# Gate tiles of the recurrent branch: from eight plain projections to a stage of block products

## The chip, the cores and the metric

The kernel runs on one core of one Trainium2 chip. The core has five engines with a queue each: TensorE (PE; its weight loads are listed apart as PEld), VectorE (DVE), ScalarE (ACT), GpSimd (POOL) and SyncE (SP), which here only issues DMAs. An engine works through its queue in order; an instruction whose input is not ready holds up all that stands behind it on that engine. SBUF holds tiles of 128 partitions; PE writes its sums into PSUM, eight banks of 128 x 512 floats here. The metric is the device time of one execution in microseconds (us), lower is better, taken as the median of several runs.

## The reference

One layer over a sequence of 1024 positions and 1024 channels. The input is normalised and modulated (`h`), and one combined projection `h @ w_in` gives the inputs of two branches and of the merge gates:

```python
hq, hf, hi, hz, gq, gk, gv, gz, ga, mg = jnp.split(h @ w_in[l], IN_OFFSETS, axis=-1)
y_h = hgrn2_branch(hq, hf, hi, hz, ...)   # 8 heads; o = linear recurrence;  rms_norm(o) * silu(hz)
y_g = gla_branch(gq, gk, gv, gz, ga, ...) # 4 heads; per-head rms_norm(o) * silu(gz)
u_h = y_h @ w_branch[l, 0]
u_g = y_g @ w_branch[l, 1]
mg = jax.nn.sigmoid(mg.reshape(B, T, 2, D_MODEL))
merged = mg[:, :, 0] * u_h + mg[:, :, 1] * u_g
x = x + gate[:, None, :] * (merged @ w_out[l])
```

and a final RMS norm. The change is about `hz`: the gate input of the recurrent branch, 1024 x 1024 like each half of `mg`. The output `o` of the recurrent branch is normalised over all 1024 channels, so the normalising factor of a position is known only when all eight heads are done; `silu(hz)` multiplies element by element and can come before or after it.

## The kernel before

All matrix products keep float32 accuracy by splitting both operands into a high and a low part of a faster type and adding three products (high x high, high x low, low x high). ACT makes the high part, DVE the low part (`split`, L195 is DVE's half).

The work has two long stretches. In the first, `Stream.go` runs a list of jobs: projections of 128 output channels (`Feat`, L454: 8 blocks of the inner dimension x 3 products x 2 halves of the sequence = 48 matmuls of 512 columns) and value blocks (`Vblk`, `Vblk2`). For each of the eight recurrent heads the list has `hq`, `hf` and, last, `hz`; for `hz` `silu_done` makes the Silu of the finished projection with a Sigmoid on ACT (L865) and a product on DVE (L866). After every six matmuls or so a job yields, and `Stream.weave` (L808) then lets two side tracks go on: `side`, the attention of the heads one after another (`attention`, L565), and `back`, preparations. Each track is a generator that yields a number of units, its distance to its next step; `PACE` = 1.1 is how many units of the side track pass with each yield of the main work. So the attention's small matmuls and its long DVE chains are spread between the projection matmuls, and where a head's steps stand in PE's queue is decided when the program is built (a scheduler may still shift an instruction by its own estimate of readiness).

A head's steps in PE's order: first score products (L596), second (L628), third (L683, L689, L694), transposes of the keys (L720), state updates (L742), outputs (L761, L763). Between them DVE multiplies in decay factors: `L592` must be done before the first step, `L624` before the second, `L672` before the third, `L748` makes the states that the outputs read. In the recurrent branch `post` then takes each half of the output out of PSUM: ACT squares it (L1007), DVE multiplies it by the norm weight and by the Silu'd gate tile (L1008), and POOL's queue stores the product to DRAM (`yh_d`, L829). POOL adds up the squares (L1019). After the eighth head `root_mean` splits the sum, adds over partitions by matmuls with `ones_r` (L876, L877), takes the root (L878), and DVE the reciprocal (L1028): the factors `rst_h`.

The back track holds `prepare`: differences of the quarters of `h` (`factors`, L1140) and sums of weight quarters (`weight_sums`, L1169 to L1173) for the second stretch, stored to DRAM by POOL (L1175). `gate_side` sums the output gate from the conditioning vector (L966), from its own place on the back track.

The second stretch, `last_stages`, computes four 1024 x 1024 products by a block scheme: each product is cut into 2 x 2 blocks and seven block products take the place of eight (`PRODUCTS`; their operands are sums and differences of quarters). A stage is 7 block products x 4 pairs of output tiles (`Pair`) x 12 matmuls = 336 matmuls (L1317). The stages in order: the gate of branch 1 (`put_gate1`), the gate of branch 0 (`put_gate0`), the branch product of `y_g` (`put_t1`) and of `y_h` (`put_m`). The first two use the same left operand `h`, so its split factors (`H[0, p]`, L1237, L1238) are kept from the first to the second. Weights come in pairs, are split by ACT (L1259) and DVE (L1260) two ahead. Before the last stage `scale_quad` (L1216) multiplies the quarters of `y_h` by `rst_h`. The side track's last head runs on inside the first stage; `scores_done` and `side_done` make PE's remaining PSUM banks (the score tile, the small tiles) available to the stages, and `seed` fills a bank with an earlier partial result.

The slot pool `S` (46 slots of 4 KB per partition) hands out all large SBUF tiles.

Of the kernel before, what the change touches and what calls it, by code (L numbers as in the profile page):

```python
# [9 lines left out]
F32 = mybir.dt.float32  # L10
# [16 lines left out]
PACE = 1.1  # L27
# [55 lines left out]
def hybrid_trunk_kernel(  # L83
# [686 lines left out]
    class Stream:  # L770


        def __init__(self):
            self.jobs = []
            self.loaded = self.prepped = 0
            self.side = deque()
            self.back = deque()
            self.hooks = {}

# [28 lines left out]
        def weave(self, units):  # L808
            for track, pace in ((self.side, PACE), (self.back, 1)):
# [188 lines left out]
    def hgrn_attention(h):  # L998
# [4 lines left out]
        def post(vh, half, po):  # L1003
            if half == 0:
                y[0], sq[0] = st.pop(("z", h)), S.get([T])
            sl = slice(half * 512, half * 512 + 512)
            nc.scalar.activation(sq[0][:, sl], po, AF.Square)  # L1007
            nc.vector.scalar_tensor_tensor(y[0][:, sl], po, vec[:, R_HN + h:R_HN + h + 1],  # L1008
                                           y[0][:, sl], ALU.mult, ALU.mult)
# [22 lines left out]
    def hgrn_v(h):  # L1032
        def done(v):
            h_state[("v", h // 4)] = v
            if h == 0:
                stream.back.append([gate_side(), 4])
        J.append(Vblk2(C_HI + h * P, done, lambda: start_side(hgrn_attention(h), 4)))

    for h in range(8):
# [9 lines left out]
        J.append(Feat(col(C_HZ + h * P), rhs_h, silu_done(h_state, ("z", h))))  # L1049
# [102 lines left out]
    sources = [[col(C_MG + n * D + d * P, 2 * P) for d in range(0, 8, 2)] for n in (1, 0)]  # L1152
    sources += [[branch(n, d) for d in range(0, 8, 2)] for n in (1, 0)]

    w_sums = [[[dp.tile([P, T], F32, name=f"ws{b}{j}{i}") for i in range(4)] for j in range(2)] for b in range(4)]
# [35 lines left out]
    GROUPS = [(b, p) for b in range(4) for p in PRODUCTS]  # L1191
    BUILT = [g for g in GROUPS if g[0] != 1]
# [3 lines left out]
    acts_of = {2: yg_d, 3: yh_d}  # L1196
    QUAD = {1: "11", 2: "21", 3: "22", 5: "11", 6: "22", 7: "12", 4: "21"}
    outs = [None] * 4
# [11 lines left out]

    def scale_quad(b, z):
        half = int(z[1]) - 1
        rst = rst_h[0][:, half * 512:half * 512 + 512].unsqueeze(1).to_broadcast([P, 2, 512])
        for t in quads[b, z]:
            v = t.rearrange("p (a t) -> p a t", a=2)
            nc.vector.tensor_mul(v, v, rst)  # L1216
# [8 lines left out]
    def build(g):  # L1225
# [4 lines left out]
        srcs = raw_f.pop(g) if b < 2 else quads[b, QUAD[p]]  # L1230
        for kk, src in enumerate(srcs):
# [7 lines left out]
            if b < 2:  # L1239
                S.free(src)  # L1240
        if b >= 2 and p in (7, 4):
# [39 lines left out]
    class Pair:  # L1281
# [25 lines left out]
        def run(self, p):  # L1307
# [4 lines left out]
            h = H[0 if self.b == 1 else self.b, p]  # L1312
# [48 lines left out]
    pairs = {(b, i): Pair(b, i) for b in range(4) for i in range(4)}  # L1361

    def last_stages():
        for n, (b, p) in enumerate(GROUPS):
# [7 lines left out]
            if b:  # L1372
                for z in H.pop((0 if b == 1 else b, p)):
# [11 lines left out]
    def put_gate1(d, half, ap, summed):  # L1385
# [3 lines left out]
        Q.free(g)  # L1389

# [40 lines left out]
    outs[:] = [put_gate1, put_gate0, put_t1, put_m]  # L1431
# [113 lines left out]
```

## Time and profile before

| | |
|---|---|
| runs | 1250.04, 1253.32, 1255.68 us; median 1253.32 |
| profiled execution | 1250.78 us; its span from first to last instruction 1249.1 us |
| mean granted clock of PE | 0.993 |
| busy share of the span | PE 96%, PEld 80%, DVE 64%, ACT 42%, POOL 11% |
| DMA | 168.82 MB, mean 135 GB/s |
| plain projections (L454) | 1632 matmuls |
| block products (L1317) | 720 + 324 + 300 = 1344 matmuls |
| first block product matmul | at 824.2 us |

The profile is of one execution. "Busy" is time in which an engine executed something; matmuls are pipelined, so the mean length of one is more than the time that one more adds. In a group's row the text reads: line, engine, operation, output <- inputs by name, shapes, count, then busy us and mean ns of one, then the idle time of the engine just before these instructions and what ended most of it. In a row of the order in time: start, length, engine, line, operation, tiles, count, and in brackets the idle time before it and what ended it. A row of windows: stretch, its length, busy time (and count) of PE, PEld, DVE, ACT, POOL, the granted clock, the share of DMA, GB/s.

### The profile page before, as it was taken

The page shows a single profiled execution, that of the slowest core. Times are in us where ns is not written, and L with a number is a line of the kernel's source. Part 1 is how long each engine was busy: PE and PEld are TensorE (multiplying, and loading weights), DVE is VectorE, ACT ScalarE, POOL GpSimd, SP SyncE. Part 2 cuts the span into 40 slices and gives each one's busy share as a digit, 9 for nine tenths or more (in the row PEclk, how much of TensorE's full clock was granted, in tenths as well). Part 3 has the DMA queues.
Part 4 walks back from the last instruction along what each step waited for, and adds up shares of the span by engine and source line. Part 5 has one row for each costly group of instructions (what it writes and reads, how often), then busy time and mean ns, then how long its engine had stood idle before and what let it go on. Part 6 is the DMA issues. An engine that isn't in the chain of part 4 may idle for free.

```text
span 1249.1 us, 20791 instructions
## 1 busy us (share of the span) xinstructions
PE 1203.5 (96%) x8603; PEld 998.8 (80%) x8603; DVE 795.9 (64%) x1239; ACT 519.1 (42%) x774; POOL 133.4 (11%) x216
## 2 busy tenths in 40 slices
PE   4899999989999999999999999999999999998997
PEld 3677899979898888788887878877888888787786
DVE  5746425695958567777884365695622668979443
ACT  4566713343334334244332323456543644454222
POOL 5510000101211022021110101011110000000000
PEclk9899999999999999999999999999999999999999
DMA  9822100652644167355342112154547556235202
GB/s 279 287 98 89 47 18 19 219 186 83 222 137 151 57 213 233 114 178 158 114 169 56 59 40 68 42 179 169 177 160 228 177 175 199 81 102 174 114 34 101
DMA packets 126928, 168.82 MB, mean 135 GB/s; under 512 B 7019, under 2 KB 97185, under 8 KB 126834
## 3 DMA queue, kind: packets, MB, share of 16 engines
q1 hardware_dynamic: 115234, 129.53, 33.2%
q0 software_dynamic: 11552, 37.97, 7.8%
q8 instruction: 67, 1.10, 0.4%
q14 instruction: 27, 0.22, 0.1%
q10 hardware_dynamic: 48, 0.01, 0.0%
HBM read 125.53 MB, written 41.94 MB: 134 GB/s over the span
## 4 chain that ended last, share of the span: by engine, by line
PE 62%; issue 22%; DVE 4%; DMA 2%; POOL 1%; ACT 1%; POOLq 0%; DVEq 0%; ACTq 0%
PE pd L454 19%; PE pd L1317 9%; PE sc_ps L1317 5%; PE pm L1317 4%; PE pd L556 2%; PE pd L558 2%; PE pd L557 2%; PE pm L761 2%; PE pm L742 2%; PE pm L763 2%; PE pd L515 1%; PE pd L514 1%; PE pd L513 1%; PE pd L1087 1%; PE pd L1089 1%
## 5 line engine op out<-in xcount | busy, mean ns | idle before, releaser
L454 PE MATMUL pd<-b,b 128*128 128x512 f32 x1632 | 387.0, 394 | 0.0
L454 PEld LDWEIGHTS pd<-b,b 128*128 128x128 f32 x1632 | 302.7, 188 | 64.5 <-issue 0.5
L1317 PE MATMUL pd<-b,b 128*128 128x512 f32 x720 | 174.1, 392 | 2.5 <-DVE b L866 1.5
L1317 PEld LDWEIGHTS pd<-b,b 128*128 128x128 f32 x720 | 133.5, 188 | 34.9 <-DVE b L866 1.9
L195 DVE TENSOR_TENSOR b<-b,b 128x1024 fp32r<-128x1024 f32 (+1 forms) x95 | 101.9, 1083 | 69.5 <-ACT b L192 36.8
L192 ACT CAST b<-b 128x1024 fp32r<-128x1024 f32 (+1 forms) x95 | 84.7, 904 | 108.4 <-DVE b L1173 16.8
L1260 DVE TENSOR_TENSOR b<-b,b 128x1024 fp32r<-128x1024 f32 x56 | 68.3, 1224 | 66.5 <-ACT b L1259 48.2
L1259 ACT CAST b<-b 128x1024 fp32r<-128x1024 f32 x56 | 58.5, 1050 | 62.4 <-PE pd L1317 17.2
L1317 PE MATMUL sc_ps<-b,b 128*128 128x512 f32 x324 | 79.0, 391 | 0.3 <-ACT scT L706 0.3
L1317 PE MATMUL pm<-b,b 128*128 128x512 f32 x300 | 72.5, 389 | 3.3 <-DVE b L1260 3.3
L513 PE MATMUL pd<-b,b 128*128 128x256 f32 x256 | 74.2, 290 | 0.0
L515 PE MATMUL pd<-b,b 128*128 128x256 f32 x256 | 72.5, 283 | 0.0
L514 PE MATMUL pd<-b,b 128*128 128x256 f32 x256 | 72.4, 283 | 0.0
L1317 PEld LDWEIGHTS sc_ps<-b,b 128*128 128x128 f32 x324 | 60.4, 188 | 13.6 <-ACT scT L706 0.7
L1317 PEld LDWEIGHTS pm<-b,b 128*128 128x128 f32 x300 | 56.3, 188 | 15.4 <-DVE b L1260 3.7
L1238 DVE TENSOR_TENSOR b<-b,b 128x1024 fp32r<-128x1024 f32 x36 | 45.0, 1260 | 15.7 <-ACT b L1237 7.9
L1175 POOL DMA_DIRECT2D ws<-b x64 | 34.7, 543 | 181.2 <-DVE b L1169 81.8
L556 PE MATMUL pd<-b,b 128*128 128x512 f32 x128 | 51.3, 401 | 0.0
L1237 ACT CAST b<-b 128x1024 fp32r<-128x1024 f32 x36 | 37.2, 1050 | 32.4 <-PE pd L1317 10.1
L557 PE MATMUL pd<-b,b 128*128 128x512 f32 x128 | 50.0, 390 | 0.0
L558 PE MATMUL pd<-b,b 128*128 128x512 f32 x128 | 49.9, 390 | 0.0
L648 ACT COPY xb<-b 128x512 f32<-128x512 f32 x48 | 29.6, 620 | 48.8 <-PE sc_ps L628 19.3
(268 smaller groups left out, 2064.8 us busy)
## 6 DMA issues: line engine op xcount, KB each, us to landing
b<-in_w_in_dram SPq DMA_DIRECT2D x66, 512.0 KB, 3.9
ws<-b POOLq DMA_DIRECT2D x64, 256.0 KB, 3.1
b<-ws SPq DMA_DIRECT2D x32, 512.0 KB, 4.4
b<-in_x_dram SPq DMA_DIRECT2D x16, 512.0 KB, 6.5
b<-in_ada_w_dram SPq DMA_DIRECT2D x32, 256.0 KB, 6.2
b<-in_w_branch_dram SPq DMA_DIRECT2D x16, 512.0 KB, 4.6
b<-h SPq DMA_DIRECT2D x14, 512.0 KB, 4.5
b<-in_w_in_dram SPq DMA_DIRECT2D x24, 256.0 KB, 3.6
```

What stands on the lines that cost most here:

```text
L192: i = nc.scalar.copy(hi, src)
L195: (eng or nc.vector).tensor_sub(lo, src, hi.bitcast(F32))
L454: nc.tensor.matmul(ps[0:w, th * 512:(th + 1) * 512], a[:, k, 0:w], b[:, th * 512:(th + 1) * 512], start=(k == 0 and n == 0), stop=(k == KT ...
L513: nc.tensor.matmul(o, lh, hi[:, k % 4, :], start=(k == 0), stop=False)
L514: nc.tensor.matmul(o, lh, lo[:, k % 4, :], start=False, stop=False)
L515: nc.tensor.matmul(o, ll, hi[:, k % 4, :], start=False, stop=(k == KT - 1))
L556: nc.tensor.matmul(o, lh, hi[:, k % 2, :], start=(k == 0), stop=False)
L557: nc.tensor.matmul(o, lh, lo[:, k % 2, :], start=False, stop=False)
L558: nc.tensor.matmul(o, ll, hi[:, k % 2, :], start=False, stop=(k == KT - 1))
L1259: nc.scalar.copy(hi, t)
L1260: nc.vector.tensor_sub(lo, t, hi.bitcast(F32))
L1317: nc.tensor.matmul(o, a[:, sl], c, start=(p in (1, 5) and kt == 0 and n == 0), stop=(kt == 3 and n == 2), skip_group_check=True)
```

## The change

The eight `hz` projections leave the job list. `hz` becomes a stage of the block scheme, the second of now five, between the two merge gates; it has the same left operand `h`, so the split factors are now kept over three stages, and `prepare` makes weight sums for it too (twenty calls in place of sixteen).

In a head, `post` no longer has a gate tile: ACT alone takes each half out of PSUM with the norm weight as a scale, and that is stored to `yh_d`. In the new stage `load_y` brings a half tile of it back, three pair runs before it is used, and `put_z` makes the Silu on ACT, multiplies the half by `rst_h`, multiplies both on DVE, and stores the result to the place it came from. The last stage then reads finished `y_h`, and `scale_quad` is gone.

With the gate stage gone from the job list there are 384 matmuls less to spread the attention over: `PACE` is 1.25 instead of 1.1, and 1.5 once the stages have begun. `gate_side` moves into `prepare`, after the weight sums of the second stage. The banks are lent to the stages in one place (`side_done`, after the third pair of the fourth product of the first stage), where two matmuls touch the score banks and all four pairs are seeded.

```diff
-PACE = 1.1
+PACE = 1.25
...
-        for track, pace in ((self.side, PACE), (self.back, 1)):
+        for track, pace in ((self.side, self.pace), (self.back, 1)):
...
             if half == 0:
-                y[0], sq[0] = st.pop(("z", h)), S.get([T])
+                y[0], sq[0] = S.get([T]), S.get([T])
             sl = slice(half * 512, half * 512 + 512)
             nc.scalar.activation(sq[0][:, sl], po, AF.Square)
-            nc.vector.scalar_tensor_tensor(y[0][:, sl], po, vec[:, R_HN + h:R_HN + h + 1],
-                                           y[0][:, sl], ALU.mult, ALU.mult)
+            nc.scalar.activation(y[0][:, sl], po, AF.Copy, scale=vec[:, R_HN + h:R_HN + h + 1])
...
-            if h == 0:
-                stream.back.append([gate_side(), 4])
...
-        J.append(Feat(col(C_HZ + h * P), rhs_h, silu_done(h_state, ("z", h))))
...
-    sources = [[col(C_MG + n * D + d * P, 2 * P) for d in range(0, 8, 2)] for n in (1, 0)]
+    sources = [[col(c0 + d * P, 2 * P) for d in range(0, 8, 2)] for c0 in (C_MG + D, C_HZ, C_MG)]
...
-        for b in range(4):
+        for b in range(5):
             for i in range(4):
                 yield from weight_sums(b, i)
+            if b == 1:
+                yield from gate_side()
...
-    BUILT = [g for g in GROUPS if g[0] != 1]
+    BUILT = [g for g in GROUPS if g[0] not in (1, 2)]
...
-    def scale_quad(b, z):
-        half = int(z[1]) - 1
-        rst = rst_h[0][:, half * 512:half * 512 + 512].unsqueeze(1).to_broadcast([P, 2, 512])
-        for t in quads[b, z]:
-            v = t.rearrange("p (a t) -> p a t", a=2)
-            nc.vector.tensor_mul(v, v, rst)
...
-            h = H[0 if self.b == 1 else self.b, p]
+            h = H[0 if self.b < 3 else self.b, p]
...
+    def part_h(d, half):
+        return yh_d[half][d // 2][:, d % 2 * 512:d % 2 * 512 + 512]
+
+    def load_y(d, half):
+        y_half[d, half] = Q.get()
+        nc.sync.dma_start(y_half[d, half], part_h(d, half))
+
+    def put_z(d, half, ap, summed):
+        g = ap if summed else Q.get()
+        y = y_half.pop((d, half))
+        nc.scalar.activation(g, ap, AF.Silu)
+        nc.vector.tensor_mul(y, y, rst_h[0][:, half * 512:half * 512 + 512])
+        nc.vector.tensor_mul(g, g, y)
+        nc.gpsimd.dma_start(part_h(d, half), g)
+        Q.free(g, y)
...
-    outs[:] = [put_gate1, put_gate0, put_t1, put_m]
+    outs[:] = [put_gate1, put_z, put_gate0, put_t1, put_m]
...
-    def scores_done():
-        while scoring or len(stream.side) > 1:
-            stream.weave(1)
-        R.lend([sc_ps[:, 0:512], sc_ps[:, 512:1024]])
-
     def side_done():
         while stream.side:
             stream.weave(1)
+        for z in (sc_ps[:, 0:512], sc_ps[:, 512:1024]):
+            nc.tensor.matmul(z, ones_r, H[0, 1][0][0].rearrange("p a t -> p (a t)")[:, 0:512], start=True, stop=True,
+                             skip_group_check=True)
+            R.lend([z])
         R.lend([mtile(), mtile()])
-        for i in (2, 3):
+        for i in range(4):
             pairs[0, i].seed()
 
-    after(0, 2, 3, scores_done)
-    for i in (0, 1):
-        after(0, 5, 3, pairs[0, i].seed)
-    after(0, 3, 1, side_done)
+    after(0, 3, 2, side_done)
+    for n, (half, odd) in ((1, (0, 0)), (4, (1, 0)), (5, (1, 1)), (6, (0, 1))):
+        for i in range(4):
+            after(1, PRODUCTS[n - 1 + (i + 1) // 4], (i + 1) % 4, lambda i=i, half=half, odd=odd: load_y(2 * i + odd, half))
...
     stream.go()
     S.free(*h_hi, *h_lo)
+    stream.pace = 1.5
```

Where the stages are numbered, the numbers of the later ones go up by one; those lines are left out.

More of the change, by code (lines that the diff above doesn't have):

```diff
@@ L778, in __init__ @@
             self.hooks = {}
+            self.pace = PACE
         def ahead(self, i, loads, preps):
@@ L1190, in hybrid_trunk_kernel @@
     raw_f, raw_w, wt = {}, {}, {}
-    GROUPS = [(b, p) for b in range(4) for p in PRODUCTS]
-    BUILT = [g for g in GROUPS if g[0] != 1]
+    GROUPS = [(b, p) for b in range(5) for p in PRODUCTS]
+    BUILT = [g for g in GROUPS if g[0] not in (1, 2)]
     X_OF = {1: (0, 0), 2: (1, 0), 4: (1, 1)}
@@ L1359, in ahead @@
             loaded[0] += 1
-    pairs = {(b, i): Pair(b, i) for b in range(4) for i in range(4)}
+    pairs = {(b, i): Pair(b, i) for b in range(5) for i in range(4)}
     def last_stages():
@@ L1454, in load_norm_w @@
         nc.sync.dma_start(fnw[0], final_norm_w.partition_broadcast(P))
[L1456 to L1463 removed]
+    after(4, 6, 3, out0.load)
+    after(4, 7, 3, load_norm_w)
+    after(4, 4, 1, out0.prep)
     def side_done():
@@ L1493, in hybrid_trunk_kernel @@
         after(b, 6, 2, last_of_all)
-    after(3, 1, 0, lambda: S.free(rst_h[0]))
     def begin():
```

30 lines of the change are left out of this document (13 added, 17 removed).

## The prediction

> **What bounds the kernel now.** I read the page first (span, busy shares, the chain), then the groups by line, then windows by stage, and last the order in time around single waits.
>
> ```profile
> span 1249.1 us, 20791 instructions
> PE 1203.5 (96%) x8603; PEld 998.8 (80%) x8603; DVE 795.9 (64%) x1239; ACT 519.1 (42%) x774; POOL 133.4 (11%) x216
> PE 62%; issue 22%; DVE 4%; DMA 2%; POOL 1%; ACT 1%; POOLq 0%; DVEq 0%; ACTq 0%
> L454 PE MATMUL pd<-b,b 128*128 128x512 f32 x1632 | 387.0, 394 | 0.0
> L1317 PE MATMUL pd<-b,b 128*128 128x512 f32 x720 | 174.1, 392 | 2.5 <-DVE b L866 1.5
> ```
>
> TensorE (PE) is busy 96% of the span and the chain that ended last is mostly PE. L454 are the projections computed as plain products (48 matmuls of 512 columns each), L1317 the block products. Their mean of 394 ns is the length of a pipelined instruction, not its price; the price is the rate at which they follow each other, and the chain in order of time has it (start, length, what, count):
>
> ```profile
> 549.16 10.93 PE pd L454 x48
> 905.32 2.72 PE pd L1317 x12
> ```
>
> 10.93/48 = 0.2277 us in the projections, 2.72/12 = 0.2267 us in the block products. By stretch (busy time of PE, PEld, DVE, ACT, POOL, then clock, DMA share, GB/s), the heads of the recurrent branch, the first block stage and the second:
>
> ```profile
> 389.50:514.00 124.50, 122.81 (x1047) 102.66 (x1050) 86.53 (x156) 45.54 (x69) 21.28 (x37) 1.00 0.51 168
> 475.00:824.00 349.00, 346.87 (x3126) 286.74 (x3125) 234.34 (x425) 130.96 (x209) 39.61 (x50) 1.00 0.36 115
> 824.00:916.00 92.00, 89.46 (x633) 71.90 (x632) 60.01 (x80) 53.53 (x79) 11.72 (x18) 1.00 0.52 171
> 916.00:992.00 76.00, 76.00 (x337) 62.96 (x336) 31.05 (x31) 35.34 (x47) 0.54 (x1) 1.00 0.60 195
> ```
>
> PE is full in all four. VectorE (DVE) has room everywhere, least in 389.5–514 (102.66 of 124.5 us), most in the second block stage (31 of 76). So a matmul less is time gained, if PE is not made to wait in its place.
>
> **The change, part by part.**
>
> *PE work.* Eight projections go: 8 x 48 x 0.2277 = 87.4 us. One block stage comes: 7 products x 4 pairs x 12 matmuls = 336 x 0.2267 = 76.2 us. Two matmuls that touch the score banks add 0.5. All of this is on the path. Net -10.7 us.
>
> *DVE, ACT, POOL, SP.* Prices:
>
> ```profile
> L866 DVE TENSOR_TENSOR b<-b,pd 128x1024 f32<-128x1024 f32 x24 | 29.3, 1223 | 12.5 <-ACT b L865 12.4
> L1216 DVE TENSOR_TENSOR b<-b,b 128x1024 f32<-128x1024 f32 x8 | 9.7, 1224 | 6.8 <-DMA b<-yh 6.8
> L1008 DVE SCALAR_TENSOR_TENSOR b<-pm,vec,b 128x512 f32<-128x512 f32 x16 | 12.0, 751 | 12.9 <-ACT b L1007 12.9
> L1260 DVE TENSOR_TENSOR b<-b,b 128x1024 fp32r<-128x1024 f32 x56 | 68.3, 1224 | 66.5 <-ACT b L1259 48.2 <-DMA gate<-b 5.6 <-PE pm L720 3.6
> L1412 DVE TENSOR_TENSOR b<-b,b 128x512 f32<-128x512 f32 x16 | 11.0, 689 | 0.1
> L1007 ACT ACTIVATE b<-pm 128x512 f32<-128x512 f32 x16 | 9.4, 597 | 26.6 <-PE pm L763 26.6
> L966 DVE SCALAR_TENSOR_TENSOR b<-b,cs,b 128x1024 f32<-128x1024 f32 x7 | 9.0, 1281 | 0.1
> ```
>
> DVE loses 8 gate products (L866, 9.8 us), 8 scalings (L1216, 9.8) and 16 output products (L1008, 12.0); it gains 14 weight splits (L1260, 17.1) and 32 half-tile products in put_z (by L1412, 22.0), both inside the new stage. If that stage looks like 916–992, DVE has 45 us free there and gets 39: covered, at cost nothing; without the cover the excess over 76 us would show one for one. The 16 output copies that ACT takes over (16 x 0.597 = 9.6 us) and 16 Silu (9.6) lie under PE too (ACT 35 of 76 us, and 131 of 349 in the head stretch). The L1216 scalings leave a stage where PE hardly waits; I give nothing for it. The sums of gate_side (L966, 9.0 us) are no new work, but in the built program they now stand in DVE's queue among the first recurrent head's state updates, in DVE's fullest stretch: 102.66 + 9.0 = 111.7 us of DVE work there. What that costs is part of the step term below.
>
> ```profile
> ws<-b POOLq DMA_DIRECT2D x64, 256.0 KB, 3.1
> b<-in_w_in_dram SPq DMA_DIRECT2D x24, 256.0 KB, 3.6
> ```
>
> The new DMAs (16 stores of weight sums, 16 stores and 16 loads of half outputs) are of these sizes. A half output is asked for three pair runs ahead, 3 x 2.72 = 8.2 us against 3.6: hidden. Behind each store on POOL's queue only other stores and the head's square sum stand. With the cover gone a late load costs at most 3.6 us; 0 to 4 in all, I take 0.
>
> *The side work moves.* The attention of a head is spread as "side work" between the matmuls, so many matmuls for each step; PACE 1.25 in place of 1.1 shortens every step. Counted in the built programs, from the first to the second score step (L596 to L628) there were 30 matmuls in ten heads of twelve and are now 24 (21 to 24 in all); from the last state matmul to the outputs (L742 to L761) mostly 18, now mostly 12. This one head of before shows what must fit in the first:
>
> ```profile
> 734.56 1.31 PE L596 MATMUL sc_ps<-xb,b 128*32 128x80 f32 x64 [0.86 <-DVE xb L592]
> 735.81 7.10 PE L454 MATMUL pd<-b,b 128*128 128x512 f32 x30
> 739.52 0.47 DVE L624 TENSOR_TENSOR xb<-xb,tot 128x256 f32<-128x256 f32 x1
> 742.84 0.89 PE L628 MATMUL sc_ps<-xb,b 128*32 128x48 f32 x64
> 748.84 0.19 DVE L672 COPY_PREDICATED blk<-mask,sc_ps 128x32 f32<-128x32 int32 x1
> 752.04 0.67 PE L683 MATMUL sc_ps<-xb 128*16 128x16 f32 x62
> ```
>
> L624 is done at 739.99 and L628 starts at 742.84: 2.85 us in hand, of which 6 matmuls (1.37) go. L672 is done at 749.03, L683 starts at 752.04: 3.0 in hand; recurrent heads mostly keep these 36 matmuls, the four GLA heads go from 36 to 30. So a quiet head still fits. An unquiet one of before did not:
>
> ```profile
> 260.89 1.23 DVE L1140 TENSOR_TENSOR b<-b,b 128x1024 f32<-128x1024 f32 x1 [2.29 <-DMA b<-h]
> 268.34 0.70 PE L683 MATMUL sc_ps<-xb 128*16 128x16 f32 x62 [2.98 <-DVE blk L672]
> 267.00:270.00 3.00, 1.66 (x106) 1.62 (x108) 3.00 (x8) 0.99 (x2) 0.26 (x1) 0.69 0.45 180
> 270.00:273.00 3.00, 3.00 (x21) 2.43 (x18) 3.00 (x6) 0.68 (x1) 0.53 (x1) 0.74 0.16 24
> ```
>
> DVE stood for a load (the prepared factors share its queue), everything behind it slipped and PE lost 2.98 us. The same collision now has up to 12 matmuls (2.7 us) less cover. Bounds for the twelve heads together: 0 (they fit) to 12 x 2 x 1.37 = 33 us (every first step and every output step loses all of its 6 matmuls). The quiet head is nearest to most: I take +2.5, about one such collision.
>
> After that stall the clock granted was 0.69 and 0.74 in two windows of 3 us: 3 x (0.31 + 0.26) = 1.7 us of lost rate. The Trainium skill ("TensorE: Matmul & The Clock Gate", Part 1: The HAM clock gate) puts the point at an idle window of about 3.4 us; here 2.98 us was enough. By that rule stalls as I expect them cost only their length; by the row a long one costs up to 1.7 more, and the sum below would be -2.7 in place of -4.4.
>
> *Waits behind the forget gate.* The second head of each four starts right behind its own forget-gate projection, whose factors pass ACT and DVE first:
>
> ```profile
> 512.02 1.23 DVE L195 TENSOR_TENSOR b<-b,b 128x1024 fp32r<-128x1024 f32 x1
> 513.95 1.31 PE L596 MATMUL sc_ps<-xb,b 128*32 128x80 f32 x64 [0.87 <-DVE xb L592]
> ```
>
> Here and at 734.56 (0.86), 30 matmuls stood between the projection and the first step, so the way through DVE took 30 x 0.2277 + 0.87 = 7.7 us, a weight split of 1.2 among it. Now 24 and 27 matmuls stand there (5.5 and 6.1 us); the split is gone from the first and gives way to one sum of some 0.7 in the second, so the way takes 6.5 and 7.2. Two waits of 1.0 and 1.1 in place of 1.73 in all: +0.3, bounds -1.7 (both go) and +1.9 (the way stays 7.7).
>
> *The end of the side work.* Before, one head ran inside the first block stage; now nearly two do, with fewer matmuls between their last steps. After the last output matmul the square sum goes over POOL and ACT back to PE, then Sqrt frees the last two banks:
>
> ```profile
> 864.88 1.08 ACT L1007 ACTIVATE b<-pm 128x512 f32<-128x512 f32 x2
> 867.11 2.56 POOL L1019 TENSOR_TENSOR b<-b,b 128x1024 f32<-128x1024 f32 x1
> 869.70 1.06 ACT L192 CAST b<-b 128x1024 fp32r<-128x1024 f32 x1 [1.17 <-POOL b L1019]
> 871.43 0.40 PE L876 MATMUL pm<-b,ones_r 128*128 128x512 f32 x1
> 872.64 0.39 PE L877 MATMUL pm<-b,ones_r 128*128 128x512 f32 x1
> 873.62 1.28 ACT L878 ACT_TABLE_LOAD   x1
> 874.91 1.27 ACT L878 ACTIVATE b<-pm,eps_t 128x512 f32<-128x512 f32 x2
> 876.53 1.13 ACT L1297 COPY pm<-b 128x512 f32<-128x512 f32 x2
> ```
>
> From 864.88 to 871.43 are 6.55 us, covered by 28 matmuls (6.3). Now 16 stand there (3.6): a wait of 2.9. From 873.03 to the first half of L1297 (877.1) are 4.1 us; now 13 matmuls stand there before a product needs that bank (2.9): 1.1. Together 4.0; 0.5 of it was paid before. Net +3.5, bounds 0 (other work fills) and 8 (both last heads lose as much).
>
> *Sum.* -10.7 + 2.5 + 0.3 + 3.5 = -4.4 us. The profiled execution took 1250.78 us (span 1249.1), so it would take 1246.4; that execution lies 2.5 under the median of the three runs (1253.32), and from the median the forecast is 1248.9.
>
> **The rivals.**
>
> *The gain holds in full.* All steps fit, the two waits behind the forget gate go and the end is filled: -10.7 - 1.7 = -12.4, 1240.9 from the median. For it: DVE's room, and a scheduler that may place matmuls of the next product into a gap. Against: the end of the side work, where the built program shows 16.
>
> *The waits eat it.* Two collisions like the one at 268 us on top of what there was, each with its clock loss: 2 x (2.7 + 1.7) = 8.8 in place of 2.5, sum +1.9, 1255.2: no measurable change. For it: twenty weight sums instead of sixteen stand in DVE's queue, and 389.5–514 gets gate_side while its matmuls come closer together.
>
> *Slower.* The short steps bind: DVE comes late in every head, and the 6 matmuls taken from a step turn into PE idle time. There are 24 such steps (first and output, twelve heads), 1.37 us each if lost in full. The rest of the sum (-10.7 + 0.3 + 3.5 = -6.9) is used up at 5 steps, and the kernel is slower by over 0.5% from 6.9 + 6.3 = 13.2 us, 10 steps. With 16 it takes 1253.3 - 6.9 + 21.9 = 1268. For it: DVE stands between PE's steps in every head, in one queue with the weight sums and splits. Against it: 2.85 us in hand in the quiet head.
>
> **How the numbers follow.** Half a per cent, 6.3 us, is about what a measurement of this kernel can tell from no change. Forecast (around -4.4, from -8 to -1): 0.42, a third of it beyond the half per cent; gain in full: 0.27; waits eat it: 0.16; slower: 0.15. Faster: 0.14 + 0.27 = 0.41. Same: 0.28 + 0.13 = 0.41. Slower: 0.15 + 0.03 = 0.18. The range goes down to the full gain (1240) and up into the slower case as far as 13 lost steps (6.9 less than 17.8, 10.9 above the median's 1253.3: 1264); what is left out is the rest of the slower case and what lies below the full gain. The forecast's own range is 1245 to 1252.
>
> **What would show it.** Right: the projections' line with 1248 matmuls, the block line with 1680, a new stage of some 76 us in which PE does not wait; waits of about 1 us behind L592 in two heads, a few us behind L672 in one or two, and one wait of about 3 us in front of the matmul with ones_r. Wrong: PE idle by DVE in head after head (L624, L672, L748), a clock under 1 in windows of the heads, DVE at 25 of 25 us through the first block stage, or PE waiting in the new stage for a Silu that stands behind a half output's load.

## The result, and the profile after

| | before | after |
|---|---|---|
| median of the runs beside each other, 4 each (us) | 1253.12 (1250.04 to 1255.68) | 1280.09 (1276.57 to 1285.79) |
| profiled execution (us) | 1250.78 | 1280.42 |
| span (us) | 1249.1 | 1278.7 |
| mean granted clock | 0.993 | 0.984 |

The changed kernel is slower: ratio 1.0227, 95% interval 1.0206 to 1.0248. 1248.9 was forecast, 1240 to 1264 given as the range; the measured time lies outside it. The page after, as far as it answers to the rows of before:

```profile
span 1278.7 us, 20944 instructions
...
PE 1205.4 (94%) x8557; PEld 996.5 (78%) x8557; DVE 813.2 (64%) x1269; ACT 539.9 (42%) x817; POOL 148.9 (12%) x248
...
PE 49%; issue 29%; DVE 8%; DMA 6%; POOL 4%; ACT 3%; SPq 1%; POOLq 0%; DVEq 0%; ACTq 0%
...
L454 PE MATMUL pd<-b,b 128*128 128x512 f32 x1248 | 303.1, 398 | 0.0
...
L1309 PE MATMUL pd<-b,b 128*128 128x512 f32 x888 | 217.6, 398 | 13.6 <-ACT b L991 4.3
```

In this kernel many line numbers have moved: up to L1390 they are up to 8 lower, behind it up to 10 higher. The block product L1317 is L1309, the weight split L1259/L1260 is L1251/L1252, the adds of the weight sums L1169 to L1173 are L1166 to L1170. The matmuls came out as counted: 1248 projections, and 888 + 408 + 384 = 1680 block products (by the bank that they write). And yet PE is busy 1205.4 us, 1.9 more than before with 46 matmuls fewer, and its share fell from 96% to 94%: it is idle more, and some of its work ran more slowly. Windows of both kernels, first before, then after, show where (from 100 us to the first block product; the first block stage):

```profile
100.00:824.20 724.20, 717.83 (x6242) 609.85 (x6241) 473.97 (x811) 275.81 (x403) 81.12 (x112) 1.00 0.37 118
824.20:916.10 91.90, 89.36 (x632) 71.81 (x631) 59.81 (x80) 53.53 (x79) 11.72 (x18) 1.00 0.51 171
```
```profile
100.00:755.00 655.00, 629.80 (x5693) 532.88 (x5692) 434.40 (x744) 251.75 (x377) 78.37 (x113) 0.99 0.40 127
755.00:870.90 115.90, 102.48 (x797) 80.90 (x796) 84.83 (x133) 66.27 (x105) 21.41 (x33) 0.97 0.61 199
```

The length less PE's busy time is idle time: 6.4 and 2.5 us before, 25.2 and 13.4 after. The clock column falls from 1.00 to 0.99 and 0.97. Added up from the single records of the granted clock, (1 - clock) x time is 1.7 and 0 us before, 6.8 and 3.4 after. Call idle time and lost clock together the loss (idle time is counted here from PE's first matmul to its last):

| loss (us) | up to 100 us | heads | first block stage | later |
|---|---|---|---|---|
| before | 25.7 | 8.1 | 2.5 | 8.4 |
| after | 26.4 | 32.0 | 16.8 | 8.4 |
| more | 0.7 | 23.9 | 14.3 | 0.0 |

With the -10.7 us that the matmuls were counted to bring: -10.7 + 0.7 + 23.9 + 14.3 = +28.2 us, against a span that is 29.6 longer. So nearly all of the difference lies between 100 us and the end of the first block stage, and it is loss, not work. PE's waits in after (what waited for what; us in all, times, longest):

```profile
PE sc_ps L628 <- DVE tot L631: 12.4, 4, 5.2
...
PE pm L742 <- ACT b L721: 6.2, 7, 1.1
PE pd L1309 <- ACT b L991: 4.3, 1, 4.3
...
PE pd L1309 <- ACT pd L1292: 3.3, 1, 3.3
PE pd L1309 <- ACT b L1281: 3.1, 1, 3.1
...
PE sc_ps L596 <- DVE xb L592: 1.5, 1, 1.5
...
PE pm L877 <- ACT b L192: 0.8, 1, 0.8
```

The first row was 1.1 us (2 times) before, the second 0.4 (once). The two worst waits of L628, DVE and PE in order of time (start, length, what, idle time in front and what ended it):

```profile
393.63 0.69 DVE L1166 TENSOR_TENSOR b<-b 128x512 f32<-128x512 f32 x1 [1.87 <-DMA yg<-b]
...
394.00 5.73 PE L454 MATMUL pd<-b,b 128*128 128x512 f32 x24
...
399.89 0.69 DVE L1170 TENSOR_TENSOR b<-b,b 128x512 f32<-128x512 f32 x1
...
400.50 0.69 DVE L623 TENSOR_TENSOR xb<-b,tot 128x512 f32<-128x512 f32 x1
...
404.31 0.42 DVE L611 COPY_PREDICATED blk<-mask,sc_ps 128x64 f32<-128x64 int32 x1
...
404.88 1.38 PE L628 MATMUL sc_ps<-xb,b 128*32 128x48 f32 x57 [5.15 <-DVE tot L631]
```
```profile
566.09 5.73 PE L454 MATMUL pd<-b,b 128*128 128x512 f32 x24
569.57 0.69 DVE L1166 TENSOR_TENSOR b<-b 128x512 f32<-128x512 f32 x1 [5.71 <-DMA b<-in_w_in_dram]
...
571.38 0.68 DVE L623 TENSOR_TENSOR xb<-b,tot 128x512 f32<-128x512 f32 x1
...
575.19 0.43 DVE L611 COPY_PREDICATED blk<-mask,sc_ps 128x64 f32<-128x64 int32 x1
...
575.77 1.51 PE L628 MATMUL sc_ps<-xb,b 128*32 128x48 f32 x64 [3.95 <-DVE tot L631]
```

L623 and L624 make the operand of L628, and L611 is the last to read the score bank that L628 writes anew; L628 follows it at 0.15 us in both places. At 394 the first score step is over, but DVE's queue holds weight sums and two splits up to 400.5 (seven adds from 393.63 on); 24 matmuls cover 5.7 us of it, and PE stands for 5.15. At 569 DVE itself has stood 5.71 us for the load of a weight sum. With each of the two came a slow clock, as the windows show (columns as above; 8 us each):

```profile
402.00:410.00 8.00, 5.12 (x77) 4.36 (x78) 7.90 (x19) 3.80 (x5) 0.00 (x0) 0.79 0.37 118
571.00:579.00 8.00, 4.05 (x73) 3.16 (x72) 7.90 (x19) 3.33 (x5) 1.71 (x4) 0.79 0.36 133
```

0.79 over 8 us is 1.7 us of lost rate, beside the 5.15 and 3.95 us of waiting.

### The profile page after: what moved, and what is told of

It is laid out like the page before. It is cut to its first block, busy times and chain, and to the rows that moved or that the text cites. A ratio compares the mean times of both kernels' runs of the same rounds, so it can differ in the third digit from the quotient of the medians.

```text
span 1278.7 us, 20944 instructions
## 1 busy us (share of the span) xinstructions
PE 1205.4 (94%) x8557; PEld 996.5 (78%) x8557; DVE 813.2 (64%) x1269; ACT 539.9 (42%) x817; POOL 148.9 (12%) x248
## 4 chain that ended last, share of the span: by engine, by line
PE 49%; issue 29%; DVE 8%; DMA 6%; POOL 4%; ACT 3%; SPq 1%; POOLq 0%; DVEq 0%; ACTq 0%
PE pd L1309 11%; PE pd L454 7%; PE sc_ps L1309 5%; PE pm L1309 5%; PE pd L371 2%; POOL ws L1172 2%; DVE scT L250 1%; PE pd L556 1%; PE pd L557 1%; PE pd L558 1%; PE pd L1086 1%; PE pd L1084 1%; PE pd L1085 1%; DMA yh<-b 1%; PE pd L348 1%
## 5 line engine op out<-in xcount | busy, mean ns | idle before, releaser
L454 PE MATMUL pd<-b,b 128*128 128x512 f32 x1248 | 303.1, 398 | 0.0
L454 PEld LDWEIGHTS pd<-b,b 128*128 128x128 f32 x1248 | 233.0, 190 | 50.5 <-issue 1.2
L1309 PE MATMUL pd<-b,b 128*128 128x512 f32 x888 | 217.6, 398 | 13.6 <-ACT b L991 4.3
L1309 PEld LDWEIGHTS pd<-b,b 128*128 128x128 f32 x888 | 167.5, 191 | 53.1 <-ACT b L991 4.7
L1252 DVE TENSOR_TENSOR b<-b,b 128x1024 fp32r<-128x1024 f32 x70 | 85.2, 1222 | 85.3 <-ACT b L1251 55.2
L195 DVE TENSOR_TENSOR b<-b,b 128x1024 fp32r<-128x1024 f32 (+1 forms) x87 | 92.0, 1068 | 73.6 <-ACT b L192 52.3
L1251 ACT CAST b<-b 128x1024 fp32r<-128x1024 f32 x70 | 72.8, 1049 | 97.9 <-PE sc_ps L1309 21.4
L1309 PE MATMUL pm<-b,b 128*128 128x512 f32 x408 | 98.4, 391 | 1.5 <-DVE b L1252 1.0
L1309 PE MATMUL sc_ps<-b,b 128*128 128x512 f32 x384 | 92.9, 390 | 0.6 <-DVE b L1296 0.6
L1309 PEld LDWEIGHTS pm<-b,b 128*128 128x128 f32 x408 | 76.8, 189 | 18.5 <-DVE b L1252 1.6
L1309 PEld LDWEIGHTS sc_ps<-b,b 128*128 128x128 f32 x384 | 71.9, 188 | 16.4 <-DVE b L1296 1.0
L1172 POOL DMA_DIRECT2D ws<-b x80 | 43.2, 541 | 244.7 <-DVE b L1166 139.2
L1230 DVE TENSOR_TENSOR b<-b,b 128x1024 fp32r<-128x1024 f32 x36 | 45.6, 1281 | 16.3 <-PE pd L1309 6.5
L556 PE MATMUL pd<-b,b 128*128 128x512 f32 x128 | 51.6, 403 | 0.0
L1229 ACT CAST b<-b 128x1024 fp32r<-128x1024 f32 x36 | 37.3, 1049 | 31.8 <-DMA b<-fx 8.7
L558 PE MATMUL pd<-b,b 128*128 128x512 f32 x128 | 49.9, 390 | 0.0
L557 PE MATMUL pd<-b,b 128*128 128x512 f32 x128 | 49.9, 390 | 0.0
L513 PEld LDWEIGHTS pd<-b,b 128*128 128x128 f32 x256 | 48.9, 191 | 0.2
```

What stands on the lines that cost most here:

```text
L195: (eng or nc.vector).tensor_sub(lo, src, hi.bitcast(F32))
L454: nc.tensor.matmul(ps[0:w, th * 512:(th + 1) * 512], a[:, k, 0:w], b[:, th * 512:(th + 1) * 512], start=(k == 0 and n == 0), stop=(k == KT ...
L513: nc.tensor.matmul(o, lh, hi[:, k % 4, :], start=(k == 0), stop=False)
L556: nc.tensor.matmul(o, lh, hi[:, k % 2, :], start=(k == 0), stop=False)
L557: nc.tensor.matmul(o, lh, lo[:, k % 2, :], start=False, stop=False)
L1172: nc.gpsimd.dma_start(w_sums[b][i // 2][q][:, i % 2 * 512:i % 2 * 512 + 512], parts[p].rearrange("p k f -> p (k f)"))
```

## The experiments

Three theories at first. A: in DVE's queue the weight sums stand in front of the heads' steps (A1: because they wait for late loads; A2: by their own 66 us of work). B: cover; 384 matmuls less lie over the heads' chains of DVE and ACT, and the steps are short. C: the loss belongs to the first block stage or to the new code. Each comparison is with runs of the kernel before on the same chip (medians 1249.3 to 1253.8).

**The adds left out.**

```diff
-        add(parts[7], x1[:, :, 0], x1[:, :, 1])
-        add(parts[5], x1[:, :, 1], x2[:, :, 1])
...
-        add(parts[6], parts[7], x2[:, :, 1])
-        add(parts[3], parts[6], x2[:, :, 0])
+        parts = {5: xs[0][:, 0:512], 6: xs[0][:, 512:1024], 3: xs[1][:, 0:512], 7: xs[1][:, 512:1024]}
```

In the changed kernel:

> The changed kernel with the adds of the weight sums left out: prepare loads the quarters and stores them unsummed, so the products 3, 5, 6 and 7 use wrong weights; loads, stores and all matmuls stay. Theory A (DVE's queue): the sums stand in front of the heads' steps and wait there for their loads; without them the PE waits at the second score step (12.4 us in the changed kernel) fall under 3, idle time of PE in the head stretch from 25 us to under 10, and with the clock that is lost behind long waits the time is 1255 to 1264. Theory B (cover): with 384 matmuls less, and the steps shortened, any chain is too long for its cover; the time stays above 1272. Theory C (the first block stage, where two heads meet the preparation of the stages): idle time in the head stretch stays, and so does the time within 4 us, unless the waits of that stage go (13 us), which gives 1262 to 1268.

and in the kernel before:

> The same in the kernel before (products 3, 5, 6, 7 use wrong weights): the control. PE waited little behind the sums there (about 1 us at the second score step), so all theories expect 1249 to 1253; if it gains as much as the changed kernel does, theory A says nothing about the change.

After without the adds took 1262.47 us (1261.7 to 1264.34), ratio to before 1.0099 [1.0079, 1.0119]: 17.6 us less than after. Before without them took 1251.0, ratio 1.0004 [0.9991, 1.0017]: nothing. The waits of L628 fell to

```profile
PE sc_ps L628 <- DVE tot L631: 1.5, 3, 0.9
```

So the same kind of work, covered in the kernel before, is not covered in the changed one. But 11.5 us remain above before, where the count has -10.7.

**PACE back to 1.1.** One line: `PACE = 1.25` to `PACE = 1.1`.

> The changed kernel with the steps of the head stretch as long as before (1.1 units per yield instead of 1.25); what is not done by then moves into the first block stage. Theory B: idle time in the head stretch falls from 25 to some 8 us, the first block stage gains 5 to 10 of idle time, time 1266 to 1274. Theory A: the waits behind late loads stay, since the loads are late by the same time, and the stage gets worse: 1278 to 1290. Theory C: the stage has three heads to hold: 1285 to 1300.

1263.6 us (1259.73 to 1267.48), ratio 1.0106 [1.0076, 1.0135]: 16.5 us less than after. Longer steps help too, and again only about half way to what the count says. The windows (heads; first block stage):

```profile
100.00:725.30 625.30, 614.02 (x5515) 522.26 (x5514) 416.23 (x716) 248.66 (x364) 70.29 (x102) 1.00 0.38 125
725.30:856.70 131.40, 114.34 (x976) 91.62 (x975) 95.27 (x156) 72.95 (x119) 27.80 (x40) 0.92 0.56 187
```

With the lost clock the loss is 11.3 us in the heads, where after has 32.0, and 27.3 in the first block stage, where after has 16.8.

**Both together.**

> The changed kernel with PACE 1.1 as before and with the adds of the weight sums left out (the quarters are stored unsummed, so the block products from them are not the reference's). If the two losses are separate, the gains of 17.6 and 16.5 us add up: 1280.1 - 34.1 = 1246, 1243 to 1249, and the change is then worth 5 us. If both edits remove the same stalls (a step fits either when DVE has nothing in front of it or when its cover is long): 1258 to 1264. Theory C (a fixed loss at the first block stage and in the new stage, which neither edit touches): 1252 to 1258.

1261.73 us (1260.04 to 1267.92), ratio 1.0095 [1.0066, 1.0125]. The gains do not add up at all. The windows of the two kernels without adds, PACE 1.25 first, then 1.1 (heads; first block stage):

```profile
100.00:743.50 643.50, 629.56 (x5704) 532.63 (x5703) 386.28 (x686) 255.55 (x380) 78.36 (x114) 0.99 0.40 130
743.50:856.60 113.10, 103.00 (x798) 81.98 (x796) 73.36 (x119) 65.81 (x104) 21.34 (x33) 0.95 0.60 201
```
```profile
100.00:720.00 620.00, 615.39 (x5521) 523.21 (x5520) 377.36 (x660) 249.41 (x361) 70.86 (x104) 1.00 0.40 129
720.00:851.80 131.80, 114.81 (x977) 92.95 (x977) 83.82 (x140) 74.39 (x123) 26.22 (x38) 0.91 0.54 180
```

Idle time in the heads falls from 13.9 to 4.6 us, and in the first block stage it grows from 10.1 to 17.0; with the lost clock 17.4 + 15.2 = 32.6 against 4.6 + 28.9 = 33.5. With PACE 1.1 the heads' steps are as long as before, so the heads end later against the matmuls, and what is left of them is pressed into the first block stage, where it has to end before the banks are lent. Without the adds PACE moves this loss from one place to the other and does not remove it. With the adds (the run before this one) it moved part of it and removed about 10 us: 38.6 in the two places against 48.8.

**The removal alone, in the kernel before.** Eight projections and their gate product leave the kernel before; nothing takes their place.

```diff
-            nc.vector.scalar_tensor_tensor(y[0][:, sl], po, vec[:, R_HN + h:R_HN + h + 1],
-                                           y[0][:, sl], ALU.mult, ALU.mult)
+            nc.scalar.activation(y[0][:, sl], po, AF.Copy, scale=vec[:, R_HN + h:R_HN + h + 1])
...
-        J.append(Feat(col(C_HZ + h * P), rhs_h, silu_done(h_state, ("z", h))))
```

With PACE 1.25:

> The kernel before without the gate projections of the recurrent branch and without the product with them (the output lacks silu(hz)), the output copied by ACT as in the changed kernel, steps of 1.25: the change's first half alone. By the matmuls alone (384 x 0.2277 = 87.4 us) 1165.7. Theory B: nearly all of the lost 27 to 38 us shows here: 1190 to 1203. Theory A with sixteen sums in place of twenty: 1180 to 1192. If the loss came with the added stage instead: 1166 to 1174.

and with PACE 1.1:

> The kernel before without the eight hz projections and the product with their Silu (ACT takes the output out of PSUM), at its own PACE 1.1; the factor silu(hz) is left out of the result. The matmuls alone give 1250.9 - 87.4 = 1163.5; with PACE 1.25 1198.6 was measured, 35 more. Theory B (the short steps are the loss): with the steps as long as before most of the 35 us go, 1165 to 1175. Rival (the loss is in taking the matmuls away, wherever the side work then stands: DVE has as much to do in 87 us less, and the heads' end moves into the first block stage): 1185 to 1200.

1198.59 us (1194.88 to 1202.73), ratio 0.9587 [0.9558, 0.9616], and 1210.45 (1207.48 to 1211.33), ratio 0.9672 [0.9654, 0.9691]. The matmuls alone would give 1163.5 and 1162.8 beside the kernel before of the same chip. The loss of 35 and 48 us is there without weight sums for a new stage, without the new stage and without the new loan of the banks. Long steps make it worse here, where in the changed kernel they took 16.5 us off; so the length of the steps by itself is not the loss (B as first put, "the short steps are the loss", falls). What is common to all of them is the matmuls that are gone.

**The cover put back.** The changed kernel, whole, with the eight projections in the job list again, their result unused:

```diff
-PACE = 1.25
+PACE = 1.1
...
         if h % 4 == 0:
             hgrn_v(h)
+        J.append(Feat(col(C_HZ + h * P), rhs_h, silu_unused))
```

> The changed kernel with the eight plain hz projections put back into the job list where they stood (Sigmoid and product are made, the result is dropped) and PACE 1.1; the new stage and all else stays. Theory B (cover: the heads' chains need these matmuls over them, wherever they then lie): the heads run as before, and the time is that of before plus the new stage, 1251 + 76.7 = 1328, 1324 to 1333; the eight projections, 87 us of work, then add only some 48 us to the changed kernel. Rival C (the loss comes from the new code: the sums in one row, the loan of the banks in one place, the new stage): the changed kernel plus 87, 1360 to 1368. In between (1335 to 1350): both.

1330.8 us (1329.65 to 1331.58), ratio 1.0634 [1.06, 1.0667], within the 1324 to 1333 of theory B. Its windows (heads; first block stage) and two of its waits:

```profile
100.00:828.10 728.10, 718.60 (x6241) 609.79 (x6240) 477.92 (x812) 283.03 (x416) 92.46 (x128) 1.00 0.40 129
828.10:921.60 93.50, 89.77 (x635) 72.23 (x634) 57.98 (x79) 55.38 (x82) 11.51 (x18) 1.00 0.52 174
```
```profile
PE pd L1316 <- ACT pd L1299: 3.1, 2, 2.9
...
PE sc_ps L628 <- DVE tot L631: 0.7, 1, 0.7
```

Idle 9.5 and 3.7 us where after has 25.2 and 13.4 (with lost clock 14.9 in all against 48.8, before 10.6), with all twenty weight sums in place. This run splits the change in two. The new stage and all that comes with it cost 1330.8 - 1249.3 = 81.5 us where 76.7 were counted. The eight projections, 87.4 us of matmuls, are worth only 1330.8 - 1280.1 = 50.7 us: 36.7 us come back as loss when they are taken away and PACE goes to 1.25. Of this, 16.5 us belong to PACE: the changed kernel at the same PACE of 1.1 took 1263.6, so there the projections are worth 67.2 us and 20.2 come back. In the kernel before, at its own PACE of 1.1, 48 came back. How much the projections serve as cover thus depends on PACE and on what else the kernel has; that they do is seen in both kernels.

**Can the sums be covered otherwise?** Four tries, nothing left out in any. The loads one sum earlier (`yield from sum_loads(n // 4, n % 4)` ahead of the adds of the sum before):

> The changed kernel, in which a weight sum's two loads are issued one sum earlier; the adds stay on DVE in the same number and in the same places between the heads' steps. Theory A1 (DVE's queue stands at the first add for a load or for the slot that it needs: 6.3 and 5.5 us of idle time in front of L1166): most of the 17.6 us that leaving out the adds gave come back, 1263 to 1268. Theory A2 (the adds' own 66 us of DVE work are what is too much between the heads' steps): no more than 4 us come back, 1276 to 1282. Theory B (cover alone): no change.

1280.52 us (1277.88 to 1281.57), ratio 1.024 [1.0221, 1.0258]: no change in the time. But the sums did not keep their places, as the expectation had them: 12 were done ahead of the first block product, where after has 17, and the last at 1017 us instead of 834. In front of the adds in the heads DVE stood 9.2 us for transfers, 19.1 in after. The loss in the heads and the first block stage together fell from 48.8 to 34.6 us, and behind the stage it grew from 8.4 to 18.0. In this build stalls went (the one at 404 us), and others came (L596 4.3 at 689, L1320 5.1 in the new stage). So earlier loads bring nothing in all, but A1 and A2 are not told apart by this run.

The adds on POOL (`add = nc.gpsimd.tensor_add`):

> The changed kernel with the adds of the weight sums on POOL in place of DVE; nothing is left out. Theory A (they stand in DVE's queue in front of the heads' steps, whether waiting or working): as with the adds left out, 1260 to 1266, and the waits of L628 for DVE fall from 12.4 us to under 3. Rival: POOL's adds are slower and its queue holds the stores and the square sums, or they slow DVE beside them: 1272 or more, and the waits move to weight sums arriving late or to L876.

1306.62 us (1305.03 to 1310.33), ratio 1.045 [1.0426, 1.0473]: 26.5 us slower than after. The longest wait of L628 is 10.3 us now. DVE's own operations became slower beside POOL's adds; rows of after, then of this one (mean ns of one behind the comma):

```profile
L748 DVE SCALAR_TENSOR_TENSOR b<-b,tot,pm 128x128 f32<-128x128 f32 x48 | 16.6, 347 | 2.7 <-PE pm L742 1.6
...
L623 DVE TENSOR_TENSOR xb<-b,tot 128x512 f32<-128x512 f32 x12 | 8.3, 695 | 12.5 <-PE sc_ps L596 12.5
...
L993 DVE TENSOR_SCALAR b<-b 128x1024 f32<-128x1024 f32 x8 | 5.5, 692 | 0.2
...
L624 DVE TENSOR_TENSOR xb<-xb,tot 128x256 f32<-128x256 f32 x12 | 5.5, 456 | 0.0
```
```profile
L748 DVE SCALAR_TENSOR_TENSOR b<-b,tot,pm 128x128 f32<-128x128 f32 x48 | 16.6, 346 | 2.7 <-PE pm L742 1.3
...
L623 DVE TENSOR_TENSOR xb<-b,tot 128x512 f32<-128x512 f32 x12 | 10.9, 905 | 25.1 <-PE sc_ps L596 25.1
...
L624 DVE TENSOR_TENSOR xb<-xb,tot 128x256 f32<-128x256 f32 x12 | 8.6, 716 | 0.0
...
L993 DVE TENSOR_SCALAR b<-b 128x1024 f32<-128x1024 f32 x8 | 7.5, 931 | 0.2
```

L623 and L624, with two inputs in SBUF, went from 695 to 905 and from 456 to 716 ns, and L993, with one, from 692 to 931; L748, whose second large input is in PSUM, did not move. These are means over all of a line; the few that ran beside a POOL add took far longer (the last section has them).

Twelve sums and gate_side behind the heads, first wrongly put (`while stream.side: yield 1` ahead of the third stage's sums):

> The changed kernel with the weight sums of the last three stages (12 of 20) and gate_side moved behind the last head, into the block stages; nothing is left out. Theory A2 (the adds' work on DVE among the heads): 12/20 of the 17.6 us that leaving the adds out gave, and some 2 for gate_side: 1280 - 12.6 = 1267.5, 1263 to 1271. Rival (the place does not matter, or the sums now collide with the splits in the block stages): 1274 to 1284, with new waits of the block products for DVE's split behind L1166.

> As the one with late sums, and the scaling of the keys of a recurrent head (one DVE pass of 0.75 us a head) is made by ACT, which has 252 of 655 us busy in the heads. If DVE's work among the heads is what counts, whatever it is: 8 x 0.75 = 6 us less of it, and at the rate of the sums (17.6 us for 66 us of adds) 1.6 us, hardly more than can be seen, 1264 to 1269. If the way behind the forget gate is the narrow place (ACT's passes in front of the first products, DVE's in front of L596): up to 5 us either way against the one with late sums.

1279.31 us (ratio 1.0224 [1.0192, 1.0256]) and 1276.78 (1.0197 [1.0151, 1.0243]): no change that can be told from after. The trace shows that the edit did not do what it was to do: the side track is empty for a moment between two heads, the sums went on there, and all twenty were done by 783 us (834 in after). Only gate_side moved, to 803 us. So these runs say nothing on the sums; moving the keys' scaling to ACT as well gave 2.5 us at most.

Then with the wait for the loan of the banks (`while not heads_over: yield 1`):

> The changed kernel with the weight sums of the last three stages (12 of 20) made behind the eighth recurrent head's end; gate_side stays where the change put it, nothing is left out. (In the one with late sums they waited only until the side track was empty for a moment between two heads, and the trace shows all twenty done by 781 us, in the heads; this one makes them wait for the loan of the banks.) Theory A2 (the adds' work on DVE among the heads): 12/20 of the 17.6 us, 1280 - 10.6 = 1269, 1264 to 1273. Rival (the block stages can't take them without waits, or the eight sums that stay are those that stand badly): 1275 to 1284.

> The same with PACE 1.1. With the adds left out, PACE made no difference (1262.5 against 1261.7): the heads lost less and the first block stage more. If that holds here too, as after_behind within 4 us. If what is left is the sums among the heads that PACE 1.1 gives room: 1258 to 1263.

1296.01 us (ratio 1.034 [1.0312, 1.0369]) and, with PACE 1.1, 1293.06 (1.0313 [1.028, 1.0346]): slower than after by 13 to 16. The heads' loss fell by 4 us only (32.0 to 27.8; the eight sums that stayed include those around 390 us, and the stall at 398 is still 5.22 long), and behind the first block stage the loss grew from 8.4 to 31.0. One of the new stalls, with what stands ahead of it on DVE and ACT:

```profile
851.32 0.54 POOL L1174 DMA_DIRECT2D ws<-b  x1 [0.66 <-DVE b L1172]
...
855.73 0.69 DVE L1169 TENSOR_TENSOR b<-b,b 128x512 f32<-128x512 f32 x1 [4.71 <-DMA b<-in_w_in_dram]
...
857.09 1.04 ACT L1256 CAST b<-b 128x1024 fp32r<-128x1024 f32 x1 [5.52 <-DVE b L1169]
...
859.62 2.07 PE L1314 MATMUL pd<-b,b 128*128 128x512 f32 x4 [4.73 <-ACT b L1256]
```

A sum's second add waits 4.71 us for its load. ACT's next high part (L1256) waits 5.52 us, and the product waits 4.73 for the one behind it. The row names that add as what released ACT, but it had ended at 856.42; the store of a sum issued at 851.32 (L1174) landed at 856.87, nearer to 857.09, so a slot that this store held is the likelier cause; it was not tested. No version that computes the whole layer beat the kernel before.

## Why the prediction was wrong

By its own steps:

- *What bounds the kernel* held: PE, and a matmul less is time gained "if PE is not made to wait in its place". That condition is what failed.
- *PE work, -10.7.* The counts held (1248 and 1680), and the sum of this term and the measured loss, +28.2, comes within 1.4 us of the span's difference.
- *DVE and ACT of the new stage, 0.* Right: DVE has 39 us of work in the 80 of it (870.9 to 951), and PE is busy for all 80.
- *The new DMAs, 0 (0 to 4).* Wrong by a little: at 956.03 PE waited 3.34 us for a seed copy (L1292) that stood on ACT behind a weight's high part, and that had waited 7.06 us for a slot that put_z's store frees. With its slow clock window it cost 5.0. What waited was not the load that I had costed but a slot held by the store; the same stall is there in the run with the cover put back (2.9).
- *Waits behind the forget gate, +0.3* (its own waits, 1.0 and 1.1 against 1.73, give +0.4). L596 waited 1.5 in all against 1.7 before: -0.2, as small as said.
- *The end of the side work, +3.5 (0 to 8).* In the place that I named the wait is 0.8 (L877). But the first block stage lost 14.3 more, beyond the bound of 8, mainly at three places I had not named: the first products waited 4.31 us for the bank of the last forget-gate projection, whose second pass on ACT (L991, at 761.15) stands behind copies that wait for DVE; at 809 they waited 3.08 us for ACT behind a factor's load; and there are short waits of the second head (L742, L628).
- *Shorter steps in the heads, +2.5 (0 to 33): this is the step that failed.* 23.9 us were measured, 18.8 of it idle time and 5.1 clock. The bounds held it, but by luck, since they counted another loss (1.37 us at each of 24 steps); the value taken did not. I took the quiet head at 734 us as the measure for most and allowed one collision, of 2.7 us at most, the matmuls that the steps lost. Two things were wrong in it. The reserve in front of the second step was measured to the wrong instruction: not L624 releases L628 but L611, which ended 0.35 us later in that head (2.50 us in hand, not 2.85) and 1.5 us later in the two below. And 734 us was one of the roomy heads. In the trace of before two others look like this:

```profile
566.21 0.47 DVE L624 TENSOR_TENSOR xb<-xb,tot 128x256 f32<-128x256 f32 x1
...
567.73 0.42 DVE L611 COPY_PREDICATED blk<-mask,sc_ps 128x64 f32<-128x64 int32 x1
...
568.30 0.89 PE L628 MATMUL sc_ps<-xb,b 128*32 128x48 f32 x64
...
569.12 0.26 DVE L631 TENSOR_TENSOR tot<-tot 128x64 f32<-128x64 f32 x1
```
```profile
611.61 0.46 DVE L624 TENSOR_TENSOR xb<-xb,tot 128x256 f32<-128x256 f32 x1
...
613.13 0.42 DVE L611 COPY_PREDICATED blk<-mask,sc_ps 128x64 f32<-128x64 int32 x1
...
613.77 0.89 PE L628 MATMUL sc_ps<-xb,b 128*32 128x48 f32 x64
```

L628 starts 0.15 and 0.22 us behind L611's end, without a wait worth a row: these heads had no reserve left (so had those at 256 and 469 us; L631 is still to come at 568, so it is not what releases). Over the twelve heads before had 0.15 to 3.0 us from L611's end to L628, after 0.06 to 1.6: most of the roomy ones gave up the 1.37 us of the six matmuls and still fit, as I had worked out for one. But four heads of twelve collided, with 5.15, 3.95, 1.94 and 1.38 us. The reserve of before does not tell which: of these four heads two had none, and the other two (5.15 and 1.38) had 2.2 and 2.8 us, while the second and the eighth head had none and now fit. What was wrong above all is the cap: which sums and splits stand in front of L623 changes too, and a load that DVE stands for is as long as it is. And seven times PE lost a little at a step that I had costed within the whole and not by itself: L742, 6.2 us in all, behind ACT's copy of the transposed keys (L721). Fewer matmuls in between do not explain it, for in four of the seven heads there were as many between the transposes and the state updates as before, or more; why ACT came later was not separated.
- *Clock.* I gave the row's price (1.7 us for a long stall) beside the sum and left it out of it. It was 11.4 us more over the whole execution (20.6 against 9.2).

Of the rivals, "slower: the short steps bind" was nearest in sign. Its picture, 24 steps that each lose up to 1.37 us, was not what happened in the heads; and the run with 1.1 and no new stage (1210.45 against 1198.59) shows that the length of the steps alone does not decide. What the runs show in its place: the matmuls of the projections are cover for the heads' work on DVE and ACT, and that cover was nearly used up. Of 87.4 us taken away, 36.7 came back as loss in the kernel as changed (20.2 with its PACE left at 1.1), with short steps more of it in the heads, with long ones in the first block stage. About 17.6 us of it goes when the weight sums' adds are left out, though not by loading them earlier, giving them to POOL or making twelve of them later. Which of the heads' own operations make up the rest was not separated.

## What to carry to other kernels

The busy share of an engine off the path (DVE at 64%) says little on whether work may be taken from the engine on the path. Look at how long each step's chain is beside what lies over it, at the worst steps and not at a quiet one, and count what other work can stand in the same queue in front of it. Where matmuls serve as cover, an experiment with the same matmuls put back, unused, and nothing else changed gives what they are worth: here 67 of 87 us at one value of PACE, and 51 when PACE changed with them.

## What the runs showed of the hardware

The granted clock fell to 0.5 for stretches of 3.41 us or multiples of it, and within a trace all of them begin on one grid of that length (404.59 and 575.26 us in after are 50 such lengths apart). Over the fifteen traces, from 100 us to 30 us ahead of the end, such a stretch began in or within 3.4 us behind 23 of 23 stalls of PE of 4 us and more, 13 of 17 of 3 to 4, 31 of 47 of 2 to 3, 5 of 25 of 1.5 to 2, and 6 of 161 of 0.6 to 1.5. Of stalls that have no other of 0.3 us or more within 7 us it was 24 of 31 for 2 to 3 us and 0 of 111 for 0.6 to 1.5. The Trainium skill ("TensorE: Matmul & The Clock Gate", Part 1: The HAM clock gate) describes a free-running window of 3413 ns, and the lengths agree; it lets the clock fall after an idle window of about 3.4 us, and by these counts a stall of 2 us is enough more often than not.

Some DVE operations ran more slowly beside two-input adds on POOL. In after_pool the two L623 that lay beside such an add for more than half of their time took 1773 and 2130 ns, where the ten that met none took 695; five L624 took 982 to 1223 against 461; and two L993, which have one SBUF input, 1640 and 1661 against 692. POOL's adds took 1437 ns in the mean. Four L748, with an input in PSUM, were not slowed (340 against 346). The Trainium skill ("GPSIMD Engine Reference", 1. Specifications) says that POOL shares its SBUF interfaces with VectorE and names two SBUF inputs as one of two cases of contention; L623 and L624 agree, and whether L993 falls under the other case (a 2-port perf mode) no run here shows. In the expectation it was the rival.
